# Entering an expert's code by one announced table branch, with shared last products behind the join and one outer branch around the overflow

## The chip, the cores and the metric

The kernel runs on one core of one Trainium2 chip, in one launch. The metric is the device time of that core in microseconds (us). Times shown are medians of several executions; the profile is one further execution, taken by the hardware profiler.

## The reference, cut to what matters

The program is two layers of a diffusion backbone over 512 latent tokens of 1024 channels. Layer 0 is a two-way recurrent mixer and a dense SwiGLU, layer 1 a short convolution and a top-2-of-8 expert SwiGLU. The change touches the expert part alone:

```python
def swiglu(h, w_gu, w_down):
    g, u = jnp.split(h @ w_gu, 2, axis=-1)
    return (jax.nn.silu(g) * u) @ w_down

def moe_swiglu(h, w_router, w_gu, w_down):
    logits = (tok @ w_router).astype(jnp.float32)
    top_v, top_e = lax.top_k(logits, TOP_K)
    gates = jax.nn.softmax(top_v, axis=-1)
...
    def expert_block(args):
        xb, e = args
        return swiglu(xb, w_gu[e], w_down[e])

    ys = lax.map(expert_block, (xs, blk_e)).reshape(n_slots, -1)
    ys = ys * slot_gate[:, None].astype(ys.dtype)
    out = jnp.zeros_like(tok).at[slot_tok].add(ys)
```

Each of the 512 tokens goes to 2 of 8 experts, and an expert's hidden width is 3584. How many of the 1024 token-expert pairs fall on an expert is known only on the chip: 128 on average, 512 at most.

## The kernel before

**Routing.** TensorE, VectorE and GpSimd work out each token's two experts, its rank within them (`dest`) and the eight counts (`cnt`). GpSimd scatters the token numbers into a table in DRAM in eight indirect DMAs, each of which waits for the one before it. SP reads the table back as `slots`, GpSimd gathers the first expert's rows (`xg`), and `prep` transposes, modulates and splits them into `x`, the high and low float32r parts of two blocks of 128 tokens.

**Weights.** An expert has 42 pieces of 1 MB: 28 of the gate and up matrix ("gu") and 14 of the down matrix ("dn"), in the order of use: two gu pieces for a group of 256 hidden units, then the dn piece of the group two back, and at the end the last two dn pieces (groups 12 and 13 of 14). SP loads them ahead into eight raw tiles. Each is then split: ScalarE casts it to the high part (L180) and VectorE subtracts that to get the low part (L181). There are three pairs of tiles for the parts (`wh0`/`wl0`, `wh1`/`wl1`, `wxh0`/`wxl0`), and `Weights` is the bookkeeping that says which piece is in which: `next` hands out a piece, gives up the one before it, and splits ahead by one piece while a pair is free (`hs` holds the pairs in use).

**An expert's code.** `expert(Wt, e, m, s0, q, nxt)` is written out for five sizes `m` (128, 144, 160, 192, 256 tokens), all for the same stretch of weights. With m = 128 (`few`) the tokens stand in the array and the weights stream; then `turn` transposes the hidden units, ScalarE and VectorE split them, and `down` multiplies them with a dn piece. With more tokens (`many`) the weights stand in the array for the gu pieces. `down` adds each group into PSUM: `yp[0]` holds the first 128 tokens, the same in all five copies, and `yp[1]` the rest of them, up to 128 more. At the end ScalarE copies `yp[0]` to an SBUF tile (L2072), VectorE `yp[1]`, and SP writes both to `ybuf`. While expert e runs, the rows of expert e + 1 are gathered and prepared (`prep` at groups 8 to 11), and its first weight pieces are loaded and split.

**How a copy is chosen.** Every engine has its own instruction stream and takes its own branches. For each expert, `arm` builds a tree of comparisons of the count with 144, then 128 or 160, then 192 (`tc.If`/`Else`); a branch that is not taken runs on, a taken one jumps over whole copies. At the end of a copy an unconditional branch leads to the join, except after the last copy (m = 128), which stands next to it. In this data the sizes that run are 128, 192, 160, 144, 144, 192, 128, 128 for experts 0 to 7. Nothing is moved across a join: what is written inside a copy stays there.

**After the experts.** For each of the eight experts there is a further copy for its tokens beyond 256, each in its own `tc.If` (L2108). No expert has that many here, so all eight are jumped over, one after the other, on every engine. Then GpSimd gathers each token's two rows of `ybuf` (L2125), and the combination, the last norm and the output follow.

Of the kernel before, what the change touches and what calls it, by code (L numbers as in the profile page):

```python
"""Two-layer RWKV-7 / short-conv / MoE backbone block on one Trainium2 core.

float32 products run as three float32r passes over an exact split of each operand
(x = H + L, H = x rounded to float32r, L = x - H, both exact in float32r), or as plain
float32 products where the shapes are small.
"""
# [23 lines left out]
D = 1024  # L30
# [5 lines left out]
E = 8  # L36
# [11 lines left out]
MOE_GROUPS = F // 256  # L48
XHL, XM, NKEY, NKK, NW, NTA, NP, NSX, NSF = 2, 1, 3, 1, 2, 2, 2, 2, 2
# which engine multiplies the channel tiles of each piece of the first adaLN matrix, and scales each tile of tokens  # L50
# [3 lines left out]
# norms work with 1 / rms times this  # L54
# [4 lines left out]
def _constants():  # L59
    """Identities and masks, which depend on shapes alone."""  # L60
# [43 lines left out]
class Weights:  # L104
    """Streams 1 MB weight pieces: DRAM -> raw tile -> float32r high and low parts."""

    def __init__(self, nc, pool, nraw):
        self.nc = nc
        self.raw = [pool.tile([128, WCOLS], F32, name=f"wraw{i}") for i in range(nraw)]
        self.items = []  # L110
        self.loaded = self.freed = self.ci = self.si = 0
        self.free, self.at = list(range(nraw)), {}
        self.hl = []
        self.hn = 0
        self.hs = {}
# [25 lines left out]
    def clone(self, items):  # L141
        """A stream of other pieces through the same tiles."""
# [4 lines left out]
        w.hs = {}  # L147
# [10 lines left out]
    def state(self):  # L158
        return self.loaded, self.freed, self.ci, self.si, self.hn, dict(self.hs), list(self.free), dict(self.at)

    def restore(self, st):
        self.loaded, self.freed, self.ci, self.si, self.hn, hs, free, at = st
        self.hs, self.free, self.at = dict(hs), list(free), dict(at)

    def split_ahead(self, ahead):
        """Splits pieces up to `ahead` after the current one while high/low slots last."""
# [19 lines left out]
    def next(self, tag):  # L186
        """High and low parts of the next piece (the one before is done with)."""
        self.hs.pop(self.ci - 1, None)
# [23 lines left out]
class Bank:  # L212
    """A PSUM tile that Plan picks when the operation that fills it is scheduled."""
# [3 lines left out]
class Plan:  # L217
    """Operations with their engines, costs and operands, issued in the order that list scheduling gives."""
    # from the issue of a DMA to its transfer, from its end to what needs it
    DMA = 0.65, 1.2  # L220
    LAG = 0.2
    # engines whose operations go in program order
# [23 lines left out]
    def lag(self, i, engine):  # L246
        """From the end of operation i to the start of one that needs it."""
# [84 lines left out]
class Build:  # L332
# [4 lines left out]
    def mm3(self, out, sh, sl, mh, ml, first, last):  # L337
        """out += (sh + sl).T @ (mh + ml) with the low-by-low term under float32's last bit."""
# [5 lines left out]
    def rsqrt(self, pool, x, n, tag):  # L344
        """x ** -0.5 for positive x [128, n]: integer seed and three Newton steps."""
# [25 lines left out]
    def plan_weights(self):  # L371
# [49 lines left out]
        def gu(e, g):  # L421
            # rows of both the gate's and the other half's columns, four row tiles at a time
# [37 lines left out]
    def startup(self):  # L460
        """Constants, adaLN columns for the time mixer, normalised and modulated inputs."""
# [63 lines left out]
        # parameters that lie along the channels, as columns  # L525
# [18 lines left out]
        # normalised tokens, channel-major  # L544
# [114 lines left out]
        # masks of the scan: [-, direction, column]  # L659
# [15 lines left out]
    def projections(self):  # L675
# [64 lines left out]
        def mix(k, n, lo):  # L740
            """h + mu (shifted h - h) = (1 - mu) h + mu shifted h, with no shifted one beyond the edges."""
# [25 lines left out]
        # ---- receptance, values, gate and the low-rank hidden units  # L767
# [3 lines left out]
        # low-rank decay and in-context rate, both directions at once  # L771
# [14 lines left out]
        # output gate, channel-major  # L786
# [10 lines left out]
        # (this tile holds the values later)  # L797
# [10 lines left out]
        # receptance (latents only)  # L808
# [14 lines left out]
        # values, token-major, even and odd heads apart  # L823
# [63 lines left out]
        # ---- keys, their normalised form, and the scan's operands  # L887
# [7 lines left out]
        # the second piece of the key weights leaves its tile to two more buffers  # L895
# [6 lines left out]
        def own(k):  # L902
            """The keys of a buffer; the spare ones wait for the weights to be read."""
# [10 lines left out]
        def channel(q, d, ki, pr, rhl, ri):  # L914
            """The scan's operands of a channel tile from its keys and their inverse norms."""
# [15 lines left out]
            for z in range(2):  # L931
# [5 lines left out]
                else:  # L937
                    # tiles in the place of the products' operands
# [922 lines left out]
    def moe(self):  # L1861
# [219 lines left out]
        for b in range(2):  # L2081
            gather(b, b)
# [79 lines left out]
```

## Time and profile before

| | |
|---|---|
| time of 3 runs | 3314.63 us median (3314.62 to 3322.37) |
| the profiled execution | span 3315.2 us from its first to its last instruction; no other time of it is given |
| busy share of TensorE / VectorE / ScalarE / GpSimd | 87% / 63% / 46% / 12% |
| experts, first to last matmul | 1824.7 to 3238.8 us |
| last copy to the first gather of the results | 3238.8 to 3274.9 us |
| combination and output | 3274.9 to 3315.2 us |

The page divides the span into 40 equal slices of 83 us; each digit is the busy share of an engine in a slice in tenths, PEclk the clock granted to TensorE in tenths of full speed, DMA the mean busy share of the sixteen DMA engines. The experts are slices 23 to 39.

```profile
PE   7998859898967999997972989999999999989890
DVE  7627766457755454446451877767677776768782
ACT  4634538766624222224220754545454454447671
PEclk7998769999978999998985999999999999989995
DMA  6343474465467454441241986677677676669882
```

TensorE is at nine tenths or more in most of these slices, and the granted clock is near full. In the rows of the trace, PE is TensorE's matmuls, DVE VectorE, ACT ScalarE, POOL GpSimd, SP SyncE. A "q" behind an engine (PEldq, ACTq) marks what its sequencer does by itself, such as branches, loads of registers and semaphore waits, which don't count as busy. In a wait, "issue" means that the engine waited for nothing that the profile shows.

### The profile page before, as it was taken

To read this page: it belongs to the slowest core of one execution; us is meant where nothing else is said; L and a number is where in the kernel's file an instruction comes from. 1 tells how busy PE (TensorE), PEld (TensorE's weight loads), DVE (VectorE), ACT (ScalarE), POOL (GpSimd) and SP (SyncE) were. 2 spreads that over 40 slices of the span, in tenths; PEclk is the share of its full clock that TensorE was granted. 3 is DMA by queue.
4 is the path that set the end of the run, shared out by engine and by line. 5 is a ranking of instruction groups with operands and counts; after the bars stand their busy time and mean duration, and the time that the engine had idled before them with its cause. 6 is when DMAs were issued, how large, how long until landed. Compare 5 with 4: busy or idle time off the path is not lost. (4 is left out here: it accounts for less than half of the span.)

```text
span 3315.2 us, 55580 instructions
## 1 busy us (share of the span) xinstructions
PE 2890.8 (87%) x22924; PEld 2463.3 (74%) x22924; DVE 2085.2 (63%) x2910; ACT 1539.5 (46%) x1921; POOL 397.5 (12%) x378
## 2 busy tenths in 40 slices
PE   7998859898967999997972989999999999989890
PEld 6696538777867888886872779988787888978680
DVE  7627766457755454446451877767677776768782
ACT  4634538766624222224220754545454454447671
POOL 2004564335520000001001000000000000000000
PEclk7998769999978999998985999999999999989995
DMA  6343474465467454441241986677677676669882
GB/s 201 106 115 100 122 157 94 84 172 149 98 214 247 146 193 144 152 159 54 100 153 27 331 291 224 216 230 233 231 235 237 236 238 218 218 210 346 303 298 89
DMA packets 531589, 610.78 MB, mean 184 GB/s; under 512 B 79380, under 2 KB 467780, under 8 KB 531172
## 3 DMA queue, kind: packets, MB, share of 16 engines
q1 hardware_dynamic: 527460, 592.91, 56.3%
q0 software_dynamic: 3712, 12.59, 1.2%
q8 instruction: 227, 3.72, 0.5%
q14 instruction: 190, 1.56, 0.2%
HBM read 547.67 MB, written 57.76 MB: 183 GB/s over the span
## 5 line engine op out<-in xcount | busy, mean ns | idle before, releaser
L181 DVE TENSOR_TENSOR wl<-wraw,wh 128x2048 fp32r<-128x2048 f32 x147 | 336.6, 2291 | 254.4 <-ACT wh L180 245.3
L180 ACT CAST wh<-wraw 128x2048 fp32r<-128x2048 f32 x147 | 280.0, 1905 | 415.2 <-PE g L341 143.0
L2037 PE MATMUL gu<-x,wh 128*128 128x384 f32 (+3 forms) x1200 | 360.3, 341 | 36.4 <-issue 36.4
L2039 PE MATMUL gu<-x,wl 128*128 128x256 f32 x1200 | 329.9, 285 | 1.8 <-issue 1.8
L180 ACT CAST wh<-wxr 128x2048 fp32r<-128x2048 f32 x112 | 214.0, 1911 | 213.1 <-PE gu L2037 67.7
L181 DVE TENSOR_TENSOR wl<-wxr,wh 128x2048 fp32r<-128x2048 f32 x112 | 256.5, 2291 | 73.9 <-ACT wh L180 72.1
L2037 PE MATMUL gu<-x,wxh 128*128 128x384 f32 (+3 forms) x1040 | 285.0, 316 | 0.0
L2039 PE MATMUL gu<-x,wxl 128*128 128x256 f32 x1040 | 275.9, 279 | 0.0
L2037 PEld LDWEIGHTS gu<-x,wh 128*128 128x128 f32 x1200 | 231.8, 193 | 55.1 <-issue 38.6
L340 PE MATMUL g<-xh,wh 128*128 128x512 f32 (+1 forms) x704 | 262.5, 373 | 0.0
L341 PE MATMUL g<-xl,wh 128*128 128x512 f32 (+1 forms) x704 | 261.6, 372 | 0.4 <-DVE xl L1705 0.4
L342 PE MATMUL g<-xh,wl 128*128 128x512 f32 (+1 forms) x704 | 261.4, 371 | 0.0
L2039 PEld LDWEIGHTS gu<-x,wl 128*128 128x128 f32 x1200 | 232.5, 194 | 4.7 <-issue 2.2
L2045 DVE TENSOR_REDUCE sl<-gu 128x192 f32<-128x384 f32 (+2 forms) x280 | 133.6, 498 | 102.8 <-PE gu L2039 102.8
L2037 PEld LDWEIGHTS gu<-x,wxh 128*128 128x128 f32 x1040 | 195.3, 188 | 0.9
L2039 PEld LDWEIGHTS gu<-x,wxl 128*128 128x128 f32 x1040 | 195.8, 188 | 0.0
L340 PE MATMUL g<-wh,bh 128*128 128x256 f32 (+1 forms) x480 | 161.8, 338 | 7.2 <-ACT wh L180 7.2
L340 PE MATMUL yp<-wh,hu 128*128 128x512 f32 x416 | 166.9, 401 | 0.0
L342 PE MATMUL yp<-wh,hu 128*128 128x512 f32 x416 | 164.3, 395 | 0.0
L341 PE MATMUL yp<-wl,hu 128*128 128x512 f32 x416 | 164.1, 394 | 0.0
L341 PE MATMUL g<-wl,bh 128*128 128x256 f32 (+1 forms) x480 | 160.9, 335 | 1.1 <-DVE wl L181 1.1
L342 PE MATMUL g<-wh,bl 128*128 128x256 f32 (+1 forms) x480 | 160.5, 335 | 0.0
(427 smaller groups left out, 6805.5 us busy)
## 6 DMA issues: line engine op xcount, KB each, us to landing
wxr<-in_moe_w_gu_dram SPq DMA_DIRECT2D x224, 512.0 KB, 4.8
wraw<-in_moe_w_gu_dram SPq DMA_DIRECT2D x170, 512.0 KB, 4.7
wxr<-in_moe_w_down_dram SPq DMA_DIRECT2D x56, 1024.0 KB, 4.9
wraw<-in_moe_w_down_dram SPq DMA_DIRECT2D x42, 1024.0 KB, 5.5
wraw<-in_mod_w_dram SPq DMA_DIRECT2D x40, 1024.0 KB, 5.3
wraw<-in_ffn_w_gu_dram SPq DMA_DIRECT2D x28, 1024.0 KB, 5.2
gtge<-in_moe_w_gu_dram SPq DMA_DIRECT2D x54, 512.0 KB, 4.6
ybuf<-zero SPq DMA_DIRECT2D x16, 1024.0 KB, 10.3
```

The costliest lines, as they stand in the source:

```text
L180: nc.scalar.copy(h[:, :n], raw[:, :n])
L181: nc.vector.tensor_sub(l[:, :n], raw[:, :n], h[:, :n])
L340: mm(out, sh, mh, start=first, stop=False)
L341: mm(out, sh, ml, start=False, stop=False)
L342: mm(out, sl, mh, start=False, stop=last)
L2037: mm(p[:, :, :n1], wh[:, k, j * 128:(j + 1) * 128], x[q][:, k0 + k, :, :n1], start=k0 + k == 0, stop=False)
L2039: mm(p[:, 0], wl[:, k, j * 128:(j + 1) * 128], x[q][:, k0 + k, 0], start=False, stop=k0 + k == KT - 1)
L2045: v.reduce_sum(t[:, 256 * o:256 * o + m], p.rearrange("p (o t) -> p t o", o=2)[:, :m], axis=AX.X)
```

## The change

1. The routing also works out for each expert the number (0 to 4) of its copy, by comparing the count with 128.5, 144.5, 160.5 and 192.5, and the largest count. They stand in `cnt` behind the counts; the register of an expert now holds the number of its copy.
2. `tc.Switch` takes the place of the tree: each engine computes the address of the copy from that number and takes one branch to it. The copies stand at equal distances, m = 128 first, and each of them, the last too, ends in a branch to the join; a hint at a copy's start names that branch.
3. `hint(e)` announces the branch of an expert's switch to each engine: once ahead of the first gather, and for each further expert behind the join of the one before it.
4. The last two `down` steps in a copy leave out the products for `yp[0]`. `rest`, behind the join, makes them, 24 matmuls, and then the copy of `yp[0]` and its DMA. Until then both dn pieces keep their tiles (`hold`, `held`, `drop`).
5. One outer `tc.If` on the largest count encloses the eight overflow copies.

Comments and docstrings are blanked too, which leaves the code as it was. The core of the diff:

```diff
+SIZES = (128, 144, 160, 192, 256)
...
-    def next(self, tag):
-        self.hs.pop(self.ci - 1, None)
+    def drop(self):
+        for i in self.held:
+            self.hs.pop(i, None)
+        self.held = set()
+
+    def next(self, tag, hold=False):
+        if self.ci - 1 not in self.held:
+            self.hs.pop(self.ci - 1, None)
+        if hold:
+            self.held.add(self.ci)
...
-            v.tensor_copy(cnt, pr[0:1, 4, :])
+            nf, arm = tb.tile([1, E], F32, name="nf"), tb.tile([1, E + 1], F32, name="arm")
+            v.tensor_copy(nf, pr[0:1, 4, :])
+            v.tensor_copy(cnt[:, :E], nf)
+            for i, m in enumerate(SIZES[:-1]):
+                if i == 0:
+                    v.tensor_scalar(arm[:, :E], nf, m + 0.5, None, op0=OP.is_gt)
+                else:
+                    v.scalar_tensor_tensor(arm[:, :E], nf, m + 0.5, arm[:, :E], op0=OP.is_gt, op1=OP.add)
+            v.reduce_max(arm[:, E:], nf, axis=AX.X)
+            v.tensor_copy(cnt[:, E:], arm)
...
-        n = [cv(cnt[0:1, e:e + 1], min_val=0, max_val=TL) for e in range(E)]
+        arm = [cv(cnt[0:1, E + e:E + e + 1], min_val=0, max_val=len(SIZES) - 1) for e in range(E)]
...
-                wh, wl = (z.rearrange("p (k c) -> p k c", c=D) for z in Wt.next("dn"))
+                wh, wl = (z.rearrange("p (k c) -> p k c", c=D) for z in Wt.next("dn", hold=gi >= MOE_GROUPS - 2))
...
-                for f, h, hs in at:
-                    self.mm3(yp[0][:, h, :], u[:, f, :128], u[:, f, 384:], wh[:, f, hs], wl[:, f, hs],
-                             first and f == 0, last and f == 1)
+                if gi < MOE_GROUPS - 2:
+                    first_rows(gi, wh, wl)
...
-            act.copy(ys[0], yp[0].rearrange("p h c -> p (h c)"))
-            nc.sync.dma_start(ybuf[s0:s0 + 128, :], ys[0])
...
+        def rest(Wt, s0):
+            for gi, i in zip((MOE_GROUPS - 2, MOE_GROUPS - 1), sorted(Wt.held)):
+                wh, wl = (z.rearrange("p (k c) -> p k c", c=D) for z in Wt.hl[Wt.hs[i]])
+                first_rows(gi, wh, wl)
+            Wt.drop()
+            act.copy(ys[0], yp[0].rearrange("p h c -> p (h c)"))
+            nc.sync.dma_start(ybuf[s0:s0 + 128, :], ys[0])
+
+        def hint(e):
+            tc.switch_hint({x: arm[e] for x in nc.engines}, len(SIZES), label=f"expert{e}")
+
+        hint(0)
...
-                with tc.If(n[e] > sizes[i - 1]) as c:
-                    arm(*sizes[i:])
-                with c.Else():
-                    arm(*sizes[:i])
-            arm(128, 144, 160, 192, 256)
+            for i in tc.Switch(arm[e], len(SIZES), hint=f"expert{e}"):
+                W.restore(st)
+                expert(W, SIZES[i], e * TL, e % 2, nxt)
+                ends.append(W.state())
...
+            if nxt is not None:
+                hint(nxt)
+            rest(W, e * TL)
...
-        for e in range(E):
-            with tc.If(n[e] > 256):
+        with tc.If(cv(cnt[0:1, 2 * E:], min_val=0, max_val=TL) > 256):
+            for e in range(E):
+                with tc.If(cv(cnt[0:1, e:e + 1], min_val=0, max_val=TL) > 256):
...
+                    expert(Wf, 256, e * TL + 256, 0, None)
+                    rest(Wf, e * TL + 256)
```

`first_rows(gi, wh, wl)` holds the products that were taken out of `down`, in the same order. What a scheduler makes of this shows in three places of the built program. Line numbers in rows of the changed program are those of the changed file: L183 is the cast that was L180, L352 to L354 are the three matmuls that were L340 to L342, L2118 is the copy that was L2072, L1963 the scatter that was L1941, L2197 the end of the file, to which switches and jumps are put down.

The first place is GpSimd's stream in the routing. `cnt` holds counts and copy numbers, `tab` is the table of token numbers, `xg` the gathered rows. Before:

```order
L1941 DMA tab<-tok,dest 4096x1 x8
L1973 DMA xg_16625<-xnd,slots 128x1024
L1973 DMA xg_16626<-xnd,slots 128x1024
L1970 TENSOR_LOAD cnt
L2099 COMPARE_AND_BRANCH x3
```

With the change (the middle of eight equal groups of three rows is left out):

```order
L1963 DMA tab<-tok,dest 4096x1
L1992 TENSOR_LOAD cnt
L2122 ISA
L2122 BRANCH_PREFETCH_HINT
...
L1992 TENSOR_LOAD cnt
L2122 ISA
L2122 BRANCH_PREFETCH_HINT
L1963 DMA tab<-tok,dest 4096x1 x7
L1995 DMA xg_16634<-xnd,slots 128x1024
L1995 DMA xg_16635<-xnd,slots 128x1024
L2197 SWITCH_STRIDE
```

All eight register loads and all eight hints, those of experts 0 to 7 in this order, stand together between the first scatter and the other seven, ahead of the first switch. The same block of eight stands in the streams of the other four engines, at the end of the routing too; behind the joins of the experts there is no further hint for a switch.

The second place is TensorE's stream at the end of expert 0 and the start of expert 1. `yp0` and `yp1` are the two halves of the result, `hu` the hidden units, `gu0` the PSUM tile of the next expert's first gu piece, which is in `wh0`/`wl0`. Before (the end of the copy for 128 tokens):

```order
L341 MATMUL yp0_16619<-wxl0_16615,hu1_16631 128x512
L342 MATMUL yp0_16619<-wxh0_16614,hu1_16631 128x512
L2099 UNCONDITIONAL_BRANCH
L1970 TENSOR_LOAD cnt_16400
L2099 COMPARE_AND_BRANCH x3
L2037 MATMUL gu0_16621<-x1_16629,wh0_11705 128x512
```

With the change (the end of the copy for 256 tokens, the last in the program; the 24 matmuls of `rest` cut to the first and the last):

```order
L354 MATMUL yp1_16629<-wxh0_16623,hu1_16640 128x512
L2197 UNCONDITIONAL_BRANCH
L352 MATMUL yp0_16628<-wh1_11707,hu0_16639 128x512
...
L354 MATMUL yp0_16628<-wxh0_16623,hu1_16640 128x512
L2197 SWITCH_STRIDE
L2197 ISA x2
L2134 BRANCH_PREFETCH_HINT
L352 MATMUL gu0_16630<-wh0_11705,x1_16638 128x512
```

The products for `yp0` now stand between the branch to the join and the table branch (the second of the two ISA rows); the register load has gone from here. The hint in the row behind it is the one for the end of the copy.

The third place is ScalarE's stream at the same join: casts of weight pieces and the copy of `yp0`. Before:

```order
L180 CAST wh0_11705<-wxr0_16382 128x2048
L2057 CAST hu1_16631<-gu2_16623 128x2x128
L180 CAST wh1_11707<-wxr1_16383 128x2048
L2072 COPY xg0_16625<-yp0_16619 128x1024
L2099 UNCONDITIONAL_BRANCH
L1970 TENSOR_LOAD cnt_16400
L2099 COMPARE_AND_BRANCH x3
L180 CAST wxh0_16614<-wxr2_16384 128x2048
```

With the change:

```order
L2073 CAST hu1_16640<-ac1_16645 128x256
L183 CAST wh0_11705<-wraw1_61 128x2048
L2197 UNCONDITIONAL_BRANCH
L2118 COPY xg0_16634<-yp0_16628 128x1024
L2197 SWITCH_STRIDE
L2197 ISA x2
L2134 BRANCH_PREFETCH_HINT
L183 CAST wh1_11707<-wraw2_62 128x2048
L183 CAST wxh0_16623<-wxr0_16382 128x2048
```

Before, the next expert's first two gu pieces were cast inside the copy; now the first one is (`wh0`), and the second (`wh1`) comes behind the copy of `yp0` and the table branch, since two of the three pairs of tiles are held for `rest`.

More of the change, by code (lines that the diff above doesn't have):

```diff
@@ L114, in __init__ @@
         self.hn = 0
-        self.hs = {}
+        self.hs, self.held = {}, set()
     def extend_raw(self, tiles):
@@ L146, in clone @@
         w.free, w.at = list(range(len(self.raw))), {}
-        w.hs = {}
+        w.hs, w.held = {}, set()
         return w
@@ L158, in state @@
     def state(self):
-        return self.loaded, self.freed, self.ci, self.si, self.hn, dict(self.hs), list(self.free), dict(self.at)
+        return (self.loaded, self.freed, self.ci, self.si, self.hn, dict(self.hs), list(self.free), dict(self.at),
+                set(self.held))
     def restore(self, st):
-        self.loaded, self.freed, self.ci, self.si, self.hn, hs, free, at = st
-        self.hs, self.free, self.at = dict(hs), list(free), dict(at)
+        self.loaded, self.freed, self.ci, self.si, self.hn, hs, free, at, held = st
+        self.hs, self.free, self.at, self.held = dict(hs), list(free), dict(at), set(held)
     def split_ahead(self, ahead):
@@ L1872, in moe @@
         slots = sb.tile([128, E * 4], I32, name="slots")
-        cnt = sb.tile([1, E], I32, name="cnt")
+        cnt = sb.tile([1, 2 * E + 1], I32, name="cnt")
         sh, sc = self.mods[:, 1, 2, :], self.mods[:, 1, 3, :]
@@ L1986, in prep, with expert @@
             v.tensor_sub(xl, xm, xh)
-        def expert(Wt, e, m, s0, q, nxt):
+        def expert(Wt, m, s0, q, nxt):
             mm = nc.tensor.matmul
@@ L2079, in expert, with first_rows @@
                 nc.sync.dma_start(ybuf[s0 + 128:s0 + 128 + r, :], ys[1][:r])
+        def first_rows(gi, wh, wl):
+            u = hu[gi % 3]
+            for h in range(2):
+                hs = slice(h * 512, (h + 1) * 512)
+                for f in range(2):
+                    self.mm3(yp[0][:, h, :], u[:, f, :128], u[:, f, 384:], wh[:, f, hs], wl[:, f, hs],
+                             gi == 0 and f == 0, gi == MOE_GROUPS - 1 and f == 1)
+        def rest(Wt, s0):
[8 more added lines that the diff above has]
+        hint(0)
         for b in range(2):
@@ L2089, in moe @@
             ends = []
-            def arm(*sizes):
-                if len(sizes) == 1:
-                    W.restore(st)
-                    expert(W, e, sizes[0], e * TL, e % 2, nxt)
-                    ends.append(W.state())
-                    return
-                i = len(sizes) // 2
-                with tc.If(n[e] > sizes[i - 1]) as c:
-                    arm(*sizes[i:])
-                with c.Else():
-                    arm(*sizes[:i])
-            arm(128, 144, 160, 192, 256)
-            assert all(z == ends[0] for z in ends)
-        for e in range(E):
-            with tc.If(n[e] > 256):
-                Wf = W.clone(W.items[self.moe_items + e * 3 * MOE_GROUPS:self.moe_items + (e + 1) * 3 * MOE_GROUPS])
-                for b in range(2):
-                    gather(b, 4 * e + 2 + b)
-                for b in range(2):
-                    for k in (0, 4):
-                        prep(b, 0, k)
-                expert(Wf, e, 256, e * TL + 256, 0, None)
+            for i in tc.Switch(arm[e], len(SIZES), hint=f"expert{e}"):
+                W.restore(st)
+                expert(W, SIZES[i], e * TL, e % 2, nxt)
+                ends.append(W.state())
+            assert all(z == ends[0] for z in ends)
+            if nxt is not None:
[4 more added lines that the diff above has]
+                with tc.If(cv(cnt[0:1, e:e + 1], min_val=0, max_val=TL) > 256):
+                    Wf = W.clone(W.items[self.moe_items + e * 3 * MOE_GROUPS:self.moe_items + (e + 1) * 3 * MOE_GROUPS])
+                    for b in range(2):
+                        gather(b, 4 * e + 2 + b)
+                    for b in range(2):
+                        for k in (0, 4):
+                            prep(b, 0, k)
+                    expert(Wf, 256, e * TL + 256, 0, None)
+                    rest(Wf, e * TL + 256)
         ms.close()
```

## The prediction

> **What bounds the kernel now.** I read the busy shares first, then TensorE's waits during the experts, then the places where these waits lie, then what its sequencer does there. The heading of the page gives the span against which every sum below is made; the first rows of TensorE's waits between 1815 and 3239 us (what, released by what: us in total, times, longest) tell what kind of wait it is:
>
> ```profile
> span 3315.2 us, 55580 instructions
> PE gu L2037 <- issue: 36.4, 5, 8.3
> PE gu L340 <- issue: 32.6, 3, 12.8
> ```
>
> Inside an expert TensorE is the bound: in a copy's own window it is busy all but a few us. These rows (stretch, length, busy us and count of PE, PEld, DVE, ACT, POOL, then granted clock, DMA share, GB/s) are experts 1, 2, 3, 5 and 7:
>
> ```profile
> 1957.00:2165.00 208.00, 205.23 (x1192) 186.39 (x1192) 148.66 (x203) 97.40 (x102) 1.88 (x2) 0.98 0.65 219
> 2172.00:2364.00 192.00, 191.01 (x1192) 168.28 (x1192) 143.39 (x203) 96.86 (x103) 1.57 (x2) 0.99 0.70 232
> 2371.00:2559.00 188.00, 187.71 (x1192) 164.90 (x1192) 139.48 (x203) 96.25 (x103) 1.07 (x2) 0.99 0.71 236
> 2761.00:2966.00 205.00, 203.40 (x1192) 185.07 (x1192) 149.20 (x203) 97.47 (x102) 3.81 (x2) 0.99 0.65 218
> 3117.00:3239.00 122.00, 121.71 (x532) 98.02 (x532) 101.00 (x68) 84.27 (x69) 0.00 (x0) 0.99 0.80 276
> ```
>
> Divided by 42 pieces, a piece takes 4.95, 4.6, 4.5, 4.9 and 2.9 us. The lost time lies between experts. The same view from each expert's last matmul until the granted clock is full again, for the seven joins:
>
> ```profile
> 1952.42:1966.90 14.48, 7.60 (x25) 6.90 (x26) 2.35 (x2) 2.91 (x2) 1.88 (x2) 0.65 0.93 314
> 2164.53:2175.10 10.57, 2.98 (x11) 2.81 (x12) 2.44 (x2) 1.90 (x1) 1.87 (x2) 0.68 0.70 224
> 2363.13:2376.50 13.37, 5.32 (x22) 5.07 (x22) 4.72 (x3) 1.90 (x1) 1.87 (x2) 0.62 0.68 215
> 2558.89:2571.10 12.21, 3.94 (x17) 3.78 (x17) 4.72 (x3) 1.90 (x1) 3.76 (x2) 0.58 0.61 200
> 2754.29:2765.60 11.31, 3.93 (x15) 3.77 (x15) 4.71 (x3) 1.90 (x1) 3.72 (x2) 0.70 0.62 200
> 2965.07:2984.10 19.03, 6.20 (x16) 4.87 (x16) 4.01 (x3) 2.55 (x2) 1.87 (x2) 0.55 0.50 165
> 3105.89:3120.60 14.71, 3.53 (x8) 2.81 (x9) 1.87 (x2) 2.91 (x2) 0.00 (x0) 0.65 0.54 184
> sum 95.68, PE 33.50 PEld 30.01 DVE 24.82 ACT 15.97 POOL 14.98; mean PE 4.79 PEld 4.29 DVE 3.55 ACT 2.28 POOL 2.14
> ```
>
> TensorE idles 95.7 − 33.5 = **62.2 us**. The granted clock of 0.55 to 0.70 says that it also ran at half speed for a while afterwards; if all of the 33.5 busy us were at half, half of them, **16.8 us**, are lost. Together the joins cost 79 us.
>
> What fills the joins are branches. Of TensorE's, the profile shows the whole stay (count, ns min/median/max, first and last start); on ScalarE it shows the start, and the next event's start gives the rest:
>
> ```profile
> L2099 PEldq COMPARE_BRANCH  x23: 65/4722/6727, 1815.7 to 3110.5; - x23
> L2099 PEldq COMPARE_BRANCH  x3: 70/4487/6482, 2358.8 to 2370.9; - x3
> L2099 PEldq COMPARE_BRANCH  x2: 6369/6538/6708, 3103.8 to 3110.5; - x2
> L2108 PEldq COMPARE_BRANCH  x8: 3344/4758/5205, 3235.2 to 3269.0; - x8
> L2108 ACTq COMPARE_BRANCH  x8: 45/45/45, 3238.8 to 3263.3; - x8
> L2108 ACTq EVENT_SEMAPHORE  x8: 17/17/17, 3242.2 to 3268.6; - x8
> q8 instruction: 227, 3.72, 0.5%
> ```
>
> A branch that runs on costs 0.07 us, one that jumps far 3.3 to 6.7. The last row, from the page's list of DMA queues, shows that instructions come in by DMA, so I call such a stay a fetch. [...] The second row is the join after expert 2: the sequencer reached its jump at 2358.8, 4.3 us before the last matmul ended at 2363.13, because queued matmuls still ran. The third is the join after expert 6, a 128-token copy: 3103.8 against 3105.89, a lead of only 2.1 us, since that end waits for the transposed hidden units.
>
> **The tail.** From the last copy to the first gather of results, and the landing times of the DMAs on `ybuf`:
>
> ```profile
> 3238.82 1.01 ACT L2072 COPY xg<-yp 128x1024 f32<-128x1024 f32 x1 [5.16 <-PE yp L342]
> 3239.86 0.34 SPq L2073 DMA_DIRECT2D ybuf<-xg  x1
> 3274.91 0.94 POOL L2125 DMA_INDIRECT yk<-ybuf,dest  x1 [298.57 <-PEq L2108]
> DMA to landing us min/median/max: 3.0/5.2/11.4
> ```
>
> 36.1 us, eight jumps in a row on each engine. With one outer jump: ScalarE reaches it at 3238.8, loads a register (0.5) and jumps (3.4 for its first outer one, 5.3 for its last; I take 4.6): 3243.9. TensorE, 2 us ahead, is done at about 3242.3. SP issues at 3239.9, its jump lies beside the landing of that DMA (median of such, last row): 3245.1, then 0.9 us of semaphores and queue: gather at 3246.0. **Gain 28.9 us**; with two fetches in the one jump 24.3, and at most 29, since the landing stays.
>
> **The seven joins, new.** Count from the end of the last matmul of `rest`, t = 0. The hints for the switches stand all eight ahead of expert 0. No row shows whether an engine keeps more than one. I take it that the last replaces the others, so that the table branch of every expert from 0 to 7 fetches like any far jump, while the jump at a copy's end, whose hint stands in the same copy, does not wait.
>
> TensorE: the 24 matmuls of `rest` give the sequencer its lead back. One fetch lies between the median of L2108, 4.76, and the longest of L2099, 6.73; near the median, 5.3. Matmuls resume at −4.3 + 5.3 + 0.3 = 1.3 after long copies, at −2.1 + 5.3 + 0.2 = 3.4 after 128-token ones (experts 0 and 6).
>
> They find one split piece, not two. The second now waits on ScalarE, behind the copy of `yp0` and the table branch:
>
> ```profile
> 2361.31 1.02 ACT L2072 COPY xg<-yp 128x1024 f32<-128x1024 f32 x1 [0.81 <-PE yp L342]
> 2371.25 1.90 ACT L180 CAST wxh<-gtge 128x2048 fp32r<-128x2048 f32 x1 [8.92 <-issue]
> 2373.51 2.29 DVE L181 TENSOR_TENSOR wxl<-gtge,wxh 128x2048 fp32r<-128x2048 f32 x1 [7.89 <-ACT wxh L180]
> ```
>
> At this join ScalarE stood 8.92 us for two fetches: 4.5 each (3.4 to 5.3 at L2108). The branch starts with the copy (3238.8 beside 3238.82 above), so: 0.3 + 4.5 + cast 1.9 + 0.1 + subtraction 2.3 + 0.1 = 9.2. VectorE's own branch ends earlier: nothing of `rest` is on it. SP is delayed too, but eight raw tiles are ahead of it. TensorE has one piece's work until 9.2 and then waits. Expert by expert, first gap plus second: 1: 3.4 + 0.85; 2: 1.3 + 3.3; 3 and 4: 1.3 + 3.4; 5: 1.3 + 3.0; 6: 1.3 + 5.0; 7: 3.4 + 2.9. Sum **35.1 us**. The gaps are about half as long as before, so I charge half the old clock loss, 8.4 (ends 0 and 16.8). Old 79.0, new 43.5: **gain 35.5 us**. With ScalarE's fetch at 3.4 the gain is 7.7 more, at 5.3 it is 5.6 less.
>
> **The entry of expert 0 and the routing.**
>
> ```profile
> 1824.71 0.77 PE L340 MATMUL gu<-wh,x 128*128 128x512 f32 x1 [8.56 <-issue]
> 1818.52 0.69 DVE L1986 TENSOR_TENSOR x<-xm,x 128x512 fp32r<-128x512 f32 x1 [0.68 <-ACT x L1985]
> 1760.87 1.19 POOL L1941 DMA_INDIRECT tab<-tok,dest  x1 [40.16 <-DVE dest L1936]
> 1766.62 0.96 POOL L1941 DMA_INDIRECT tab<-tok,dest  x1 [4.56 <-DMA tab<-tok,dest]
> L1970 POOLq TENSOR_LOAD <-cnt x8: 290/294/495, 1802.2 to 2974.7; - x8
> L1970 SPq FUSED_REGOPS  x8: 147/147/181, 1759.2 to 1763.3; - x8
> 1758.45 0.15 DVE L1925 CAST cnt<-pr 1x8 int32<-1x8 f32 x1 [5.94 <-PE pr L1924]
> ```
>
> TensorE took two far jumps from 1815.7 on (the first L2099 row). With one it starts when both the jump (1815.2 + 4.7) and `x` (1818.5 + 0.7) are there, near 1819.9: 4.8 us earlier. Against this stand seven more small operations on VectorE ahead of the scatter, some 0.15 us each, 1 us; and on GpSimd eight loads, register operations and hints between the first and the second scatter. No row has a hint; priced as a register operation, 8 × (0.3 + 2 × 0.15) = 4.8 us beside the 4.56 us in which GpSimd waits for the first scatter anyway: 0.5 us with its queue. Hints of 1 us would make that 7. On the other engines these rows stand in the wait for the table. **Gain 3.3 us** (from −3.5 to 4.8).
>
> **Sum**: 28.9 + 35.5 + 3.3 = 67.7 off the span, 3315.2 to 3247.5. The median of the runs lies 0.6 us below the span, so 3247 us. The 24 matmuls of `rest` are moved, not added. All ends above at once, clock loss and two fetches in the tail among them, give 3229 to 3272.
>
> **Rivals.** *All hints are kept.* For: they are issued long before the branches. Against: eight in one go, 200 us apart in use, and a copy's own hint in between. [...]
>
> *No hint does anything, a copy's end included.* Each end costs a fetch of 4.7. After long copies the queue hides it but for 0.5 (five times, 2.5). After 128-token copies only two transposes are queued: 4.4 each, three times, 13.2. With 3 us of clock: 3266 us. [...]
>
> *Table branches fetch twice*, for the copy's start and for what follows: 4.5 × 7 + 4 at the entry, 3283 us. Against: untaken branches behind a far jump cost 0.07.
>
> *The other side: the second piece.* Every us by which ScalarE's table branch exceeds 4.5 is one us of TensorE's wait at each of seven joins. From 14.2 us a branch the whole gain is gone, at 17 the time is 3335 us. For: two tiles less at the join, as the rows of the program show. Against: no single fetch in the rows is over 6.7. Between 12.8 and 15.6 us nothing could be told from before.
>
> **Chances**: forecast 0.60, no hint 0.20, all hints 0.08, two fetches 0.06, no change to be measured 0.03, slower 0.03. The range, 3230 to 3278, holds the first two, 0.80, with the ends of their costs. About 0.3%, 10 us, is what a measurement of this kernel can tell from no change; faster by more 0.94, within 0.03, slower 0.03.
>
> **What the new profile would show.** One far jump at L2144, and the first gather some 7 us after the last copy. At each join two idle stretches of TensorE, 1 to 3 us released by "issue" and 1 to 5 us released by a cast or subtraction of a weight piece. If the second is missing, hints work; if there is one ahead of `rest` after experts 0, 6 and 7, the ends' hints don't. Wrong would be a GpSimd scatter chain longer by several us, or a table branch on TensorE well over 7.

## The result and the profile after

The changed kernel takes **3239.54 us** (median of 4 runs, 3236.84 to 3249.54) against 3318.50 for the one before in the same runs: ratio 0.976, 95% interval 0.9738 to 0.9782. The forecast was 3247, range 3230 to 3278. The profiled execution has this heading and, on its page, this line on the engines and this one on the instruction queue:

```profile
span 3235.0 us, 55842 instructions
PE 2887.0 (89%) x22924; PEld 2456.2 (76%) x22924; DVE 2082.2 (64%) x2917; ACT 1538.5 (48%) x1921; POOL 404.7 (13%) x378
q8 instruction: 200, 3.28, 0.4%
```

The span is 80.1 us shorter (before rounding). TensorE's arithmetic is the same, 22924 matmuls in both, and the instruction queue brought 200 packets, 27 less. First the view of stretches over the experts, from the first product with weights to the last (columns as in the prediction); before on the first line, after on the second:

```profile
1824.71:3238.82 1414.11, 1346.82 (x7588) 1167.71 (x7588) 1057.88 (x1269) 757.02 (x736) 15.07 (x12) 0.97 0.75 252
```

```profile
1816.73:3187.92 1371.19, 1340.34 (x7588) 1158.40 (x7588) 1056.12 (x1269) 755.33 (x736) 24.45 (x12) 0.99 0.78 260
```

Length less busy time is idle: 67.3 us before, **30.8 after**, 36.4 less; busy time fell by 6.5. Now what TensorE waits for in the changed kernel's experts (what, released by what: us in total, times, longest):

```profile
PE yp L2033 <- DVE hu L2075: 9.9, 5, 2.0
PE gu L2061 <- issue: 8.9, 5, 3.8
PE gu L2063 <- DVE wl L184: 4.0, 3, 1.5
PE gu L352 <- DVE xm L2004: 2.7, 4, 0.9
PE gu L352 <- ACT wxh L183: 2.6, 2, 1.3
PE yp L354 <- DVE hu L2082: 2.4, 2, 1.2
```

The fourth and sixth row stood there before. The 69.0 us of "issue" in the two rows that the prediction shows (8.6 of them at the entry of expert 0) have become 8.9, behind the moved products; the wait at that entry is now 3.2. New are 6.6 us for the second piece (third and fifth row), which the prediction had, and 9.9 us for the hidden units at the ends of the five long copies, which it had not. TensorE's branches at three joins, each with the jump at a copy's end and the table branch behind the moved products (ns shortest/median/longest, starts): into expert 1, out of a 128-token copy; into 2; and into 6, which is a 128-token copy again:

```profile
L2197 PEldq COMPARE_BRANCH  x2: 426/3146/5867, 1935.4 to 1941.3; - x2
L2197 PEldq COMPARE_BRANCH  x2: 422/2447/4472, 2145.2 to 2149.5; - x2
L2197 PEldq COMPARE_BRANCH  x2: 423/590/758, 2928.7 to 2933.1; - x2
```

In each row the shorter is the jump and the longer the table branch. All eight end jumps take 0.3 to 0.4 us (before, those of the five long copies took 4.5 to 4.7 and the 128-token copies had none), the table branches into 1 to 5 take 5.87, 4.47, 3.80, 3.58 and 3.84, those into 6 and 7 only 0.76 and 0.69. On ScalarE the table branch takes 5.4 us into 1, 2.5 to 2.7 into 2 to 5 and 0.4 into 6 and 7. The tail, from ScalarE's last copy to GpSimd's first gather:

```profile
3187.92 1.01 ACT L2118 COPY xg<-yp 128x1024 f32<-128x1024 f32 x1 [5.15 <-PE yp L354]
```

```profile
3194.33 0.94 POOL L2164 DMA_INDIRECT yk<-ybuf,dest  x1 [248.87 <-SPq L2144]
```

6.4 us where 36.1 were. Term by term (us; the last row, work ahead of any changed code, differs from run to run):

| term | forecast | profile |
|---|---|---|
| tail | 28.9 | 29.7 |
| joins, idle | 27.1 | 36.4 |
| joins, clock (all busy time of the experts) | 8.4 | 6.5 |
| routing and entry of expert 0 | 3.3 | 5.5 |
| combination | 0 | -0.5 |
| ahead of the change | 0 | 2.5 |
| sum | 67.7 | 80.1 |

### The profile page after: what moved, and what is told of

Same layout as the page of the kernel before. It is cut to its first block, busy times and chain, and to the rows that moved or that the text cites. A ratio compares the mean times of both kernels' runs of the same rounds, so it can differ in the third digit from the quotient of the medians.

```text
span 3235.0 us, 55842 instructions
## 1 busy us (share of the span) xinstructions
PE 2887.0 (89%) x22924; PEld 2456.2 (76%) x22924; DVE 2082.2 (64%) x2917; ACT 1538.5 (48%) x1921; POOL 404.7 (13%) x378
## 5 line engine op out<-in xcount | busy, mean ns | idle before, releaser
L183 ACT CAST wh<-wraw 128x2048 fp32r<-128x2048 f32 x147 | 279.9, 1905 | 392.2 <-PE g L353 149.6
L2061 PE MATMUL gu<-x,wh 128*128 128x384 f32 (+3 forms) x1200 | 350.9, 334 | 8.9 <-issue 8.9
L183 ACT CAST wh<-wxr 128x2048 fp32r<-128x2048 f32 x112 | 214.1, 1911 | 175.6 <-PE yp L2033 55.4
L352 PE MATMUL g<-xh,wh 128*128 128x512 f32 (+1 forms) x704 | 262.3, 373 | 0.0
L354 PE MATMUL g<-xh,wl 128*128 128x512 f32 (+1 forms) x704 | 261.2, 371 | 0.0
L1995 POOL DMA_INDIRECT xg<-xnd,slots x16 | 28.2, 1766 | 1126.5 <-ACT wh L183 387.6
L352 PE MATMUL g<-wh,bh 128*128 128x256 f32 (+1 forms) x480 | 161.7, 338 | 7.2 <-ACT wh L183 7.2
L352 PE MATMUL yp<-wh,hu 128*128 128x512 f32 x416 | 167.8, 403 | 0.0
L354 PE MATMUL yp<-wh,hu 128*128 128x512 f32 x416 | 165.0, 397 | 0.0
```

The costliest lines, as they stand in the source:

```text
L183: nc.scalar.copy(h[:, :n], raw[:, :n])
L352: mm(out, sh, mh, start=first, stop=False)
L354: mm(out, sl, mh, start=False, stop=last)
L1995: g.indirect_dma_start(out=xg[b], out_offset=None, in_=xnd, in_offset=bass.IndirectOffsetOnAxis(ap=slots[:, col:col + 1], axis=0))
L2061: mm(p[:, :, :n1], wh[:, k, j * 128:(j + 1) * 128], x[q][:, k0 + k, :, :n1], start=k0 + k == 0, stop=False)
```

## The experiments

The idle time is TensorE's in the experts, by the same view of one profile each.

| version | median us | ratio to before, 95% | idle us |
|---|---|---|---|
| changed kernel | 3239.54 | 0.976, 0.9738 to 0.9782 | 30.8 |
| outer branch alone | 3279.45 | 0.9888, 0.9864 to 0.9912 | 69.9 |
| no switch announced | 3246.09 | 0.9783, 0.9759 to 0.9808 | 33.9 |
| copies in opposite order | 3253.39 | 0.9803, 0.9772 to 0.9833 | 38.1 |
| announced behind the join | 3240.02 | 0.977, 0.9751 to 0.9789 | 31.6 |
| announced inside the copy | 3268.08 | 0.9858, 0.9832 to 0.9885 | 51.5 |
| nothing moved behind the join | 3234.58 | 0.9745, 0.9726 to 0.9764 | 32.3 |
| the same, not announced | 3240.13 | 0.9778, 0.9755 to 0.9801 | 31.8 |
| one piece moved | 3249.59 | 0.9783, 0.9757 to 0.981 | 39.8 |
| four tile pairs | 3237.77 | 0.9769, 0.974 to 0.9797 | 29.6 |
| 18 of 24 products moved | 3236.49 | 0.9747, 0.9721 to 0.9772 | 28.8 |
| announced in the copy on ScalarE | 3239.74 | 0.9764, 0.9744 to 0.9784 | 30.6 |
| the last two together | 3238.53 | 0.9762, 0.9746 to 0.9778 | 34.2 |

**The outer branch alone**, in the kernel before:

```diff
+        with tc.If(cv(cnt[0:1, E:], min_val=0, max_val=TL) > 256):
-        for e in range(E):
-            with tc.If(n[e] > 256):
+            for e in range(E):
+                with tc.If(n[e] > 256):
...
```

> The kernel before with nothing but the outer branch around the eight overflow branches, on the largest count. Theory: the tail's gain belongs to this edit alone. In the changed kernel's trace the first gather starts 6.4 us behind the last copy, in the one before 36.1 us; so here the first gather comes 6 to 8 us behind the last copy, the joins stay as they were (62 us idle), and the span falls by 28 to 30 us, to some 3286 us, ratio 0.991. Rival: part of that gain needs the products behind the last join, which cover TensorE's branch; then the gain stays near 24 us and the time near 3291.

The same two events of its trace, and the stretch of its experts:

```profile
3228.90 1.01 ACT L2075 COPY xg<-yp 128x1024 f32<-128x1024 f32 x1 [5.10 <-PE yp L342]
```

```profile
3235.23 0.93 POOL L2129 DMA_INDIRECT yk<-ybuf,dest  x1 [266.83 <-SPq L2110]
1824.87:3229.00 1404.13, 1334.21 (x7588) 1164.17 (x7588) 1057.44 (x1269) 757.76 (x736) 14.09 (x12) 0.97 0.76 254
```

6.3 us, so the tail's 29.8 us belong to this edit, without any moved product; the rival falls. The time fell by more (the interval is 29 to 45 us), and the last row shows where that lies: experts of unchanged code with 69.9 us of idle time, but 12.6 us less busy than before. So busy time is no measure of an edit here to better than some 10 us, and I compare idle time and single branches from here on.

**No announcements**: `hint(0)`, `hint(nxt)` and the label at the switch are deleted.

> The changed kernel without any announcement of the switches (the hint in each copy for its own end stays). Theory: the eight announcements that stand together ahead of expert 0 do nothing for the table branches; those of TensorE stay as in the changed kernel's trace, 3.6 to 5.9 us into experts 1 to 5 and 0.7 to 0.8 into 6 and 7, and the time is the same within 10 us (3230 to 3250). Rival: the last announcement is kept and is what makes the entries of experts 6 and 7 quick; then both rise to some 4 us on TensorE and to 2.5 or more on ScalarE, and the time by 5 to 10 us.

Idle time is 3 us more, and the intervals overlap. TensorE's far branches into 1 to 5 are 6.55, 4.26, 3.41, 3.30 and 3.53 us, as before within their spread; ScalarE's into 6 and 7 stay at 0.4. TensorE's into 6 rose to 3.51, as the rival has it, but that into 7 fell to 0.41. The eight announcements bought nothing that the time shows.

**Opposite order of the copies:**

```diff
-SIZES = (128, 144, 160, 192, 256)
+SIZES = (256, 192, 160, 144, 128)
...
-                    v.tensor_scalar(arm[:, :E], nf, m + 0.5, None, op0=OP.is_gt)
+                    v.tensor_scalar(arm[:, :E], nf, m + 0.5, None, op0=OP.is_le)
```

> The changed kernel with the five copies of an expert in the opposite order, 256 tokens first and 128 last, so that no expert uses the copy that stands right behind its table branch. Theory: the entries of experts 6 and 7 were quick (TensorE 0.76 and 0.69 us, ScalarE 0.4) because the code of the 128-token copy comes next in memory; here they cost what the others do, 3.6 to 5.9 us on TensorE and 2.5 to 5.4 on ScalarE, TensorE waits some 2 to 5 us more at each of these two joins and some 2 at the entry of expert 0, 6 to 12 us in all: 3243 to 3250. Rival: the announcements make them quick; then they stay at 0.7 and the time does not move.

TensorE's jump and table branch into 6, then into 7:

```profile
L2197 PEldq COMPARE_BRANCH  x2: 418/2466/4513, 2936.8 to 2941.3; - x2
L2197 PEldq COMPARE_BRANCH  x2: 418/3140/5863, 3068.8 to 3074.8; - x2
```

0.76 and 0.69 have become 4.51 and 5.86, ScalarE's 0.4 have become 2.5 and 5.7, the idle time grew by 7.3 us. So these two entries were quick only with the 128-token copy right behind its table branch. Standing there is not enough: into 6 it took 3.51 us without announcements, and into 6 and 7 it takes 4.78 and 5.61 in the version with nothing moved (below), where the branch comes 0.3 us behind the end of the jump and the one packet of the instruction queue in its stay starts 2.2 and 3.1 us behind it.

**Announced behind the join.** VectorE writes the next expert's number to a tile of its own inside each copy, and the register is loaded from it at the announcement, which therefore can't be moved ahead of expert 0:

```diff
+                if nxt is not None and gi == 4:
+                    v.tensor_copy(cur[nxt % 2], cnt[0:1, E + nxt:E + nxt + 1])
...
         def hint(e):
+            z = cur[e % 2] if e else cnt[0:1, E:E + 1]
+            arm[e] = cv(z, min_val=0, max_val=len(SIZES) - 1)
```

> The changed kernel with each expert's number copied by VectorE inside the copy before, so that the load of the register, and with it the announcement, comes right behind the join and ahead of the moved products, not eight in a row ahead of expert 0. Theory: an engine keeps one announcement, and one that is given behind the join is used; TensorE's table branches into experts 1 to 5 fall from 3.6 to 5.9 us to under 2.5, ScalarE's from 2.5 to 5.4 to under 1, and of the 15 us of gaps that follow the moved products at the seven joins 8 to 13 go: some 3227. Against it stand a register load and a wait on every engine at each join, some 0.5 us. Rival: a table branch can't be announced at all; the branches keep their length and the time is the same or up to 5 us more.

The theory falls: the far branches are 6.02, 3.39, 3.80, 3.70 and 3.49 us on TensorE. ScalarE reached its announcement 5.6 us ahead of the branch into 1 and 11.7 to 12.5 ahead of those into 2 to 5, and they still take 5.5, 2.6, 2.5, 2.8 and 2.5 us.

**Announced inside the copy**, behind the announcement of the copy's own end:

```diff
+                if nxt is not None and gi == 12:
+                    hint(nxt)
...
-            if nxt is not None:
-                hint(nxt)
             rest(W, e * TL)
```

> The changed kernel with the announcement of the next expert's switch given inside each copy, behind the copy's own announcement of its end, and none ahead of expert 0 but the first; the table branch's register is loaded again behind the join. Theory: an engine keeps one announcement, and the one that works is that of a copy's end. The later one replaces it: TensorE's jumps at the ends of copies 0 to 6 rise from 0.4 to 3.5 to 5 us, that of copy 7, where nothing follows, stays near 0.3; the table branches stay at 3.5 to 6 us. At a long copy's end some 1.2 us of matmuls are queued, so about 3.4 us more are idle at each of five joins, 2.5 at the two others: some 22 us more, 3262 us. Rival 1: the ends are quick for another reason; then the time stays at 3240. Rival 2: the table branch is announced with enough lead here and becomes quick (under 1 us); then the second half of each join gains 1 to 4 us and the time is 3245 to 3255.

TensorE's jump and table branch into expert 4, then what it waits for in all experts:

```profile
L2205 PEldq COMPARE_BRANCH  x2: 330/3000/5669, 2536.7 to 2546.0; - x2
PE yp L352 <- issue: 30.6, 7, 5.4
PE yp L2037 <- DVE hu L2079: 9.9, 5, 2.0
PE gu L2067 <- DVE wl L184: 2.9, 5, 0.9
...
PE gu L2065 <- issue: 0.4, 1, 0.4
```

The roles are exchanged: the jump at the copy's end takes 5.67 us, the table branch 0.33. All seven end jumps rose, to 5.4 to 6.5 us, and TensorE idles 30.6 us ahead of the moved products. On ScalarE all seven table branches take 0.4 us. On TensorE those into 2, 4 and 5 take 0.3 to 0.4, the other four 2.7 to 3.8. So at all seven ends the later announcement took the place of the earlier (5.4 to 6.5 us where the jump had taken 0.4), **and a table branch can be announced**: inside the copy, with 0.4 us at seven of seven entries on ScalarE and 0.3 to 0.4 at three of seven on TensorE. My theory that it can't was wrong; rival 2 is right on ScalarE and on three of seven entries of TensorE. The 8.9 us of waits behind the moved products are 0.4 here (last row), so in these versions one of TensorE's two far branches at a join was hidden, not both.

The trace has the packets of the instruction queue too. This table, put together from it, has the first three packets of 16 KB on this queue, q8, around a join, which fit TensorE's branches alone (us; stays in brackets):

| version, into expert | packets start at | jump at the copy's end | table branch |
|---|---|---|---|
| changed, 2 | 2134.97, 2147.77, 2151.60 | 2145.17 (0.42) | 2149.47 (4.47) |
| announced behind the join, 2 | 2133.46, 2146.30, 2150.12 | 2143.68 (0.41) | 2149.03 (3.39) |
| announced inside the copy, 4 | 2527.68, 2539.94, 2543.09 | 2536.72 (5.67) | 2545.98 (0.33) |
| nothing moved, 2 | 2145.07, 2158.48, 2159.10 | 2155.45 (0.34) | 2156.19 (6.59) |

Where the end is the last thing announced, the first packet starts 10.2 to 10.4 us ahead of the jump, and the jump takes 0.34 to 0.42 us. The next packet starts 2.6 to 3.0 us behind the start of the jump, whether the join announces anything or not, and a further one 1.1 to 2.9 us behind that of the table branch, which takes 3.39 to 6.59. In the third row, where the switch is announced after the end, the first packet starts 9.0 us ahead of the jump, yet the jump takes 5.67 us, with a packet 3.2 us behind its start (2539.94); the one after that (2543.09) starts 2.9 us ahead of the table branch, which takes 0.33. The packets carry no address in the trace, so it does not show what an announcement changes about them. Nor is a packet ahead of the table branch enough: in the third version, into 3 and 6, one came behind that of the jump too (2348.51, 2948.36), ahead of the branch, and the branch still took 3.8 and 3.3 us. Why stays open.

**Nothing moved behind the join:**

```diff
-                if gi < MOE_GROUPS - 2:
-                    first_rows(gi, wh, wl)
+                first_rows(gi, wh, wl)
```

with the pieces not held, and only the copy of `yp0` and its store left in `rest`.

> The changed kernel with the 24 shared products of the last two pieces back in each copy, in their old place; only the copy of yp0 and its store stay behind the join. Theory: moving them gains nothing net. In the changed kernel's trace each of the five long copies waits 1.97 us at its end for the last hidden units, which those products used to cover, and TensorE waits another 1.1 to 1.5 us for a second piece whose tile they held. Both go here (some 10 and 6 us). The table branch is still hidden by queued matmuls after long copies but for about 1 us (0.4 for the jump, 0.4 to get to the branch, 3.6 to 4.5 for it, less a lead of 4.2); the entry of expert 1, after a 128-token copy, rises to 4 to 5 us. Idle time at the seven joins 8 to 10 us instead of 25: some 3223 us, ratio to before 0.971. Rival: the products do hide the branch; without them each far branch shows 3 to 5 us, the joins come to 25 us or more, and the time is 3240 or above.

```profile
PE gu L2060 <- issue: 18.5, 5, 6.2
PE gu L352 <- ACT wxh L183: 4.0, 1, 4.0
```

The wait for the hidden units at the long copies' ends is gone, as expected, but the first gaps are 6.2, 3.4, 3.0, 3.1, 2.8, 1.5 and 4.0 us, 24 where I expected 8 to 10 (the last of them, the second row, for ScalarE's split). The table branch stands 0.4 us behind the jump here and takes 6.2 to 7.8 us into 1 to 5: in the last row of the table two packets start in its stay (2158.48 and 2159.10), where the changed kernel has one (2151.60). So the moved products do hide a branch (8.9 us of waits behind them, 24 here), and give the gain back at the two new waits: 30.8 us idle with them, 32.3 without, and the intervals overlap. Without announcements as well:

> No products moved behind the join, and no switch announced (the hint in each copy for its own end stays, the table branch and the outer branch too). Theory: both parts are idle or cost something, so this is no slower than the version without moved products: some 3220 to 3226 us, and the entry of expert 0 on TensorE is as quick as in the version without announcements (0.36 us for its table branch, 3.8 in the changed kernel). Rival: announcements help where no product stands between join and table branch; then this is 5 to 15 us slower than with them.

No slower that could be told (31.8 us idle), and TensorE is idle 1.8 us at the entry of expert 0 instead of 2.9.

**One piece moved** (12 products), the last:

> The changed kernel with only the 12 shared products of the last piece behind the join, those of the last but one in the copy. Theory: the wait of 1.97 us at the end of a long copy is covered by the 12 products of the last but one piece, a third tile pair lets the second piece be split ahead, and the 12 products behind the join (some 4.4 us) still give the sequencer its lead; the first gap at each join stays as in the changed kernel (3.75 us at expert 1, 2.0 down to 0.7 at 2 to 5, 0 at 6 and 7): idle time at the joins 9 to 10 us: some 3223 us. Rival: the second piece waits on ScalarE as before (1.1 to 1.5 us at six joins) or the wait of 1.97 us stays; then 3230 to 3236.

```profile
PE gu L2061 <- issue: 17.9, 5, 5.3
PE yp L354 <- DVE wl L184: 15.2, 5, 3.0
```

A miss. The wait for the hidden units went, but the third of the moved products waits 3.0 us at five joins for a subtraction of a weight piece that it does not read (second row). In the built program it waits, at the join behind expert 2, until VectorE has counted to 2224; the 128-token copy reaches that number with its hidden units, the copies for 144 to 256 tokens only with that subtraction. Code behind a join is shared, so its wait has one number that must do for every copy. And the branch, delayed by this to 5.7 us behind the jump, takes 5.7 to 6.7 us into 2 to 5. The distance alone does not set that: without announcements the branch into 4 comes 6.1 us behind the jump and takes 3.3. Why it is so long here stays open.

**A fourth tile pair** in place of two raw tiles, and **6 of the 24 products back in the copy**:

> The changed kernel with a fourth pair of tiles for split pieces, in the place of two of the eight raw tiles. Theory: the second piece waits behind the join because the moved products still hold two of three pairs; with a fourth it is split inside the copy, and TensorE's waits for it (4.0 us for VectorE, 2.6 us for ScalarE in the changed kernel) go: 6 to 7 us less idle, some 3233 us. Rival: a split that is now issued at the copy's end delays the last hidden units, or makes the moved products wait for VectorE as in the version with one held piece (3 us at five joins), or six raw tiles are too few and waits on DMAs appear; then 3240 to 3260.

> The changed kernel with 6 of the 24 moved products (one half of the columns of the last but one piece) back in the copy. Theory: they cover 1.4 of the 1.97 us for which a long copy waits for its last hidden units, and the 18 products that stay behind the join (4.1 us) still hide as much of the table branch as the queue allows: TensorE's wait for the hidden units falls from 9.9 to 3 us, the rest of the waits stays: 3233 us. [...]

```profile
PE gu L2061 <- DVE sl L2069: 8.5, 8, 1.3
```

```profile
PE gu L2063 <- issue: 12.7, 5, 4.6
PE yp L354 <- DVE xg L2102: 3.5, 5, 0.7
PE yp L2035 <- DVE hu L2077: 3.4, 5, 0.7
```

Both did what they were made for, and both waits came back elsewhere. With four pairs the second piece no longer waits, but TensorE waits 8.5 us for VectorE's sums inside the copies (first row). With 18 products the hidden units cost 3.4 us instead of 9.9, as the theory had it, but the branch 12.7 instead of 8.9, and VectorE's `xg` 3.5, which is the shared wait number again (in the built program the copies for 144 to 192 tokens reach it only with their last sum into `xg`, the one for 256 with the copy). 1.2 and 2.0 us less idle is all that is left of 6 to 7. The far branches themselves take 3.9 to 4.6 us into 2 to 5 there (3.6 to 4.5 in the changed kernel). The new waits stood in neither theory.

**The switch announced inside the copy on ScalarE alone**, without and with the 18 products:

> The changed kernel with the next expert's switch announced inside each copy on ScalarE alone, and no switch announced on the other engines, which keep the announcement of a copy's end. [...] TensorE's jumps and branches stay as in the changed kernel (0.4, and 3.4 to 6 for the far ones); its waits for the second piece of a 256- or 144- to 192-token copy (4.0 us for VectorE) nearly go, those of 2.6 us at experts 6 and 7, where ScalarE's branch was quick already, stay: 3 to 5 us less idle, 3235 us. Rival: ScalarE's end jump comes to delay the copy of yp0; then the waits stay and the time is 3239 to 3245.

> The same, with 6 of the 24 moved products back in the copy as well. Theory: the two gains add: of 30 us of TensorE's waits in the experts, 3 to 5 go at the second piece and some 2 to 6 at the hidden units, what is left being the table branches: 24 to 27 us idle, 3230 us, the fastest of these versions, though by less than runs of one kernel differ. Rival: the quicker ScalarE only leaves the wait to TensorE's own branch (12.7 us with 18 products); then the idle time stays at 28 us and the time at 3236.

ScalarE's branches into 2 to 5 fell to the 0.4 us that all seven take where every engine announces inside the copy (that into 6 was there already), and the 4.0 us at the second piece went, as expected. But those out of a 128-token copy, into 1 and 7, take 4.5 and 4.0, and at 7, where it had been 0.4, TensorE waits 4.0 us for ScalarE. So these two entries, though announced inside the copy, were not quick. The idle time is 30.6 us, and with the 18 products 34.2 where 24 to 27 were expected: TensorE's own branches cost 14.5 of it. No version is faster than the changed kernel by more than the measurement tells.

## Why the prediction was right, step by step

- **Tail**: right in mechanism and size, 28.9 against 29.7, and shown alone by the outer branch.
- **"The last replaces the others"**: right as far as times show it. With eight announcements ahead of expert 0 the table branches into 1 to 5 take 3.58 to 5.87 us on TensorE, with none 3.30 to 6.55, announced behind the join 3.39 to 6.02, so the rival *all hints are kept* falls. The jump at a copy's end takes 0.3 to 0.4 us, and 5.4 to 6.5 where the next switch is announced behind it, so *no hint does anything* (3266) falls too.
- **First gap.** Experts 1 to 5: 3.4, 1.3, 1.3, 1.3, 1.3 forecast, 3.75, 1.97, 1.31, 1.13, 0.72 measured. Experts 6 and 7: 1.3 and 3.4 forecast, none measured. The step that failed is "the table branch of every expert from 0 to 7 fetches like any far jump": with the 128-token copy next behind the branch, TensorE's took 0.76 and 0.69 us into 6 and 7, in the opposite order 4.51 and 5.86.
- **Second gap**: the mechanism was right, the size was not: 21.8 us forecast, 6.6 measured. I priced ScalarE's branch at 4.5 us from a wait of 8.92 for two fetches. It took 2.5 to 2.7 into 2 to 5 and 0.4 into 6 and 7, only into 1 more (5.4). That the two fetches of 8.92 are not equal could be read from the trace before: on ScalarE 2.7 us lie between the first jump and the next event there, 6.2 between the far branch and the next. The "other side", over 14.2 us a branch, was nowhere near.
- **"The 24 matmuls of `rest` are moved, not added"**: failed by what they had covered. At a long copy's end TensorE waits 1.97 us for the last hidden units; the 12 products of the last but one piece used to lie beside VectorE's work on them. 9.9 us that the sum lacked, offset by the two errors above. Together the forecast had 35.1 us of these waits and the profile has 25.4; that errors of 4, 15 and 10 us left so little is luck.
- **Clock**: 8.4 forecast. The 6.5 us less busy time can't decide it, since a run of the same code varies by more. The clock itself can: in the stretches with a granted clock of 0.50 behind the entry of expert 0, TensorE was busy 33.7 us in the experts before and 16.6 after. By the half that the prediction charges, 16.8 and 8.3 us are lost, 8.5 less. The size was right.
- **Entry and routing**: 3.3 forecast, 5.5 measured. TensorE's wait went from 8.56 to 3.18 us, since its branch took 3.77, not 4.7 (the first product starts 0.26 us behind it). The scatter was not delayed: from the last routing product to the first transposition it is 48.19 us before and 48.06 after.
- *Table branches fetch twice* did not occur in the changed kernel: one packet starts in each stay into 1 to 5 (2151.60 in that into 2). Two in one stay occur where nothing stands between the jump and the branch: 2158.48 and 2159.10, in the version with nothing moved.

## What to carry to other kernels

Here a jump to far code took mostly 2.5 to 7.8 us. An announcement inside a copy hid TensorE's jumps at the copies' ends (0.3 to 0.4 us, but for that of the last copy in the two versions with 18 products, 3.6) or, of the next switch, table branches at all seven joins on ScalarE (0.4 us; five of seven where ScalarE's alone were announced) but at three of seven on TensorE, and there never both at a join; in a row ahead of the experts, or behind the join, the switches' announcements did nothing that the runs show. So count the far jumps at a join first, remove the ones that can be merged (here the tail, the one part whose gain an experiment shows alone), and try the likeliest target right behind its branch (0.76 and 0.69 us in the changed kernel, 4.51 and 5.86 in the opposite order, though 3.51 to 5.61 at three such entries of other versions). The 24 products between two jumps in a row made the second shorter (3.58 to 5.87 us, 6.2 to 7.8 without), but gained nothing in all.

Work that is moved behind a join to hide a branch is missing where it stood: look at what it covered, which tiles it keeps, and that its waits hold for every copy ahead of it.

## What was not expected of the hardware

After 0.76 and 0.69 us into experts 6 and 7 I expected TensorE's entry into expert 0 to be quick as well, since the 128-token copy stands right behind that branch too. This is its table branch in the changed kernel, then without announcements:

```profile
L2197 PEldq COMPARE_BRANCH  x1: 3767/3767/3767, 1812.7 to 1812.7; - x1
```

```profile
L2191 PEldq COMPARE_BRANCH  x1: 357/357/357, 1818.3 to 1818.3; - x1
```

In all five versions with the order of the change and eight announcements ahead of expert 0 it takes 3.2 to 3.8 us; where none or only that of expert 0 is given, 0.35 to 0.38 us in six. In the changed kernel a packet starts 1.0 us behind this branch, without announcements none in its stay. Why is not shown: the eight announcements also move the code behind them. It costs little here, since TensorE waits for VectorE there as well: its gap is 3.2 us with and 1.8 without. Why TensorE's entry of expert 6 took 0.76 us in the changed kernel and 3.51 without announcements stays open too.
